# Decays of a gated DeltaNet kept head by head in DRAM and broadcast into the decay tiles themselves

## The chip, the cores and the metric

The kernel runs on one core of one Trainium2 chip. The metric is the device time of one execution in microseconds (us), the median of several runs. The core has a matrix engine (TensorE, PE in the rows), a vector engine (VectorE, DVE), a scalar engine (ScalarE, ACT), GpSimd (POOL) and SyncE (SP), which here only issues transfers; ACT issues some too (ACTq). Each engine works through its own list of instructions in a fixed order, and an instruction that waits holds up everything behind it in that list.

## The reference, cut to what matters

One encoder layer: a SwiGLU feed-forward block, a mixer, a second feed-forward block. The change lies in the mixer's branch B, a gated DeltaNet with 8 heads, run in both directions. Per head and direction the decays `g` are summed up inside each chunk, and the chunk matrices are weighted with the exponential of differences of these sums:

```python
g = jnp.cumsum(g, axis=-1)
decay = jnp.exp(jnp.where(incl, g[..., :, None] - g[..., None, :], -jnp.inf))
a_mat = jnp.where(strict, jnp.einsum('bhnid,bhnjd->bhnij', k_beta, k) * decay, 0.0)
attn = jnp.einsum('bhnid,bhnjd->bhnij', q, k) * decay
```

So each head needs, for 2 directions and 4 chunks of 128 positions, the sums once as a column (one per partition) and once as a row that all 128 partitions hold.

## The kernel before, in words

The sequence has T = 512 positions, the width is 1024. Every product is split into three matrix passes of 128x512 (lines 186, 187, 188: `hi` times `uh`, `lo` times `uh`, `hi` times `ul`), so that a weight tile `raw` comes by a transfer (line 169), is rounded to `hi` by ACT (line 174) and its rest `lo` made by DVE (line 176). Three `raw` tiles and three pairs `hi`, `lo` are in rotation.

In the mixer, the eight heads are built by the generator `build`, which `EMIT`, a table of steps, interleaves with the other generators (scan, place, gates); heads are counted below by the order of their decay transfers. The tile framework then orders the instructions by priority, so that each engine's list is fixed when the program is built. `build(hd)` goes through these steps:

- three projections with short convolution (line 444 on DVE): `cq`, `ck`, `cv`;
- SiLU to `qT`, `kT`, `vT` (ACT), and the transfer of the decay rows: `Gb`, 128 x 8 x 128, one buffer (lines 468, 469);
- `tok`: transposes on PE into the bank `tp` (line 479), of which there is one; ACT empties it (lines 481, 484);
- `st`, small columns: lines 514 and 516 on DVE read the last element of each row of `Gb`, and line 517 (ACT) takes the exponential;
- `ef` and `eb`, the decay matrices of the two directions: line 528 on DVE subtracts the column from `Gb` (eight instructions of 128x128), then ACT (lines 531 to 533) and, for `eb`, POOL (line 534);
- PE makes `k k^T` and `k q^T` in the bank `o`, again one, two chunks at a time (lines 547, 548); DVE multiplies with the decay matrices into `nl` (line 552) and `at` (line 556). The second two chunks on PE must wait until `at` has read the first two out of `o`.

The row form of the decays comes from `grow` in DRAM: G is transposed on PE to `gt`, 64 rows of 128 (direction, chunk, head), and stored by one transfer (line 424) in the middle of the mixer's start. `Gb` of a head reads eight pieces of 512 bytes out of it for every partition. SP's list holds the weights, `Gb`, and the transfers of the triangular inverse (`dl`, `A`, `da`, `t`).

Of the kernel before, what the change touches and what calls it, by code (L numbers as in the profile page):

```python
# [7 lines left out]
F32 = mybir.dt.float32  # L8
# [8 lines left out]
P = 128  # L17
# [5 lines left out]
NC = T // P  # L23
H = 8
# [29 lines left out]
def tile_layer(  # L54
# [23 lines left out]
    nc = tc.nc  # L78
    pe, act, dve, pool = nc.tensor, nc.scalar, nc.vector, nc.gpsimd

    def open_pool(stack, name, bufs=1, **kw):
        if "space" not in kw:
            kw["reuse_waits"] = "tile"
        return stack.enter_context(tc.tile_pool(name=name, bufs=bufs, **kw))
# [27 lines left out]
    h = open_pool(first, "big", side="right").tile([P, KT, T], F32, tag="big", name="h")  # L112
# [206 lines left out]
    def mixer(st, u, h, post):  # L319
# [3 lines left out]
        scr = open_pool(st, "scr", bufs=2, space=DRAM)  # L323
# [10 lines left out]
        def project(i):  # L334
            made.add(i)
            if i in early:
                return early[i]
            ps = bank()
            product(ps, weight(w_in[i], KT), u, 0, KT, True, True)
            return ps  # L340
# [3 lines left out]
        wk = open_pool(dn, "wk", bufs=2)  # L344
        one = open_pool(dn, "one", bufs=1)
        with ExitStack() as dd:
            beta = dnc.tile([P, NC, 16], F32, name="beta")
            G = dnc.tile([P, 2, NC, H], F32, name="G")
# [17 lines left out]
            def early_half(t0, t1):  # L366
                for i, w in ew.items():
                    if t0 == 0:
                        early[i] = bank()
                    product(early[i], w, u, 0, KT, True, True, t0, t1)  # L370
# [15 lines left out]
            x = dt.tile([P, NC, 16], F32, tag="spx", name="spx")  # L386
# [21 lines left out]
            for d in range(2):  # L408
                dve.scalar_tensor_tensor(
                    out=g[:, d], in0=x[:, :, d * H : d * H + H], scalar=-1.0,  # L410
# [9 lines left out]
            pe.transpose(ps[0:64, 0:P], G[:].rearrange("p d c h -> p (d c h)"), ident[:])  # L420
            gt = dt.tile([64, P], F32, tag="gt", name="gt")
            act.copy(gt[:], ps[0:64, 0:P])
            grow = scr.tile([2 * NC, H, P], F32, tag="grow", name="grow")
            nc.sync.dma_start(grow[:].rearrange("a h p -> (a h) p"), gt[:])
            early_half(T // 2, T)

        with dn:
# [8 lines left out]
            def taps(acc, src, w, n):  # L436

                mid = n // 2
                act.activation(out=acc[:], in_=src[:], func=ACT.Copy, scale=w[:, mid : mid + 1])  # L439
                for i in range(n):  # L440
                    o = i - mid
                    lo, hi = max(0, -o), T - max(0, o)
                    if o:
                        dve.scalar_tensor_tensor(out=acc[:, lo:hi], in0=src[:, lo + o : hi + o],  # L444
                                                 scalar=w[:, i : i + 1], in1=acc[:, lo:hi], op0=ALU.mult,
                                                 op1=ALU.add)

            def short_conv(i):

                ps = project(12 + i)  # L450
                acc = cp.tile([P, T], F32, tag="cacc", name="cacc")
                taps(acc, ps, cvd_sb[:, i], 5)
                return acc

            def build(hd, s):
                cq = short_conv(hd)
                yield
                ck = short_conv(8 + hd)
                yield
                cv = short_conv(16 + hd)  # L460
                yield
# [3 lines left out]
                act.activation(out=kT[:], in_=ck[:], func=ACT.Silu)  # L465
                vT = cv
                act.activation(out=vT[:], in_=cv[:], func=ACT.Silu)
                Gb = wk.tile([P, 8, P], F32, tag="Gb", bufs=1, name="Gb")
                nc.sync.dma_start(Gb[:], grow[:, hd, :].unsqueeze(0).to_broadcast([P, 8, P]))

                yield

                ss = slot.tile([P, 2, NC], F32, tag="ss", name="ss")
# [28 lines left out]
                ns, sb, nr, wj, el = (st_[:, 2], st_[:, 3, 0:NC], st_[:, 4], st_[:, 5], st_[:, 6])  # L502
# [8 lines left out]
                dve.tensor_mul(brk, beta[:, :, hd], rk)  # L511
                for d in range(2):
                    last = (P - 1, 0)[d]
                    dve.tensor_sub(wj[:, d * NC : d * NC + NC], Gb[:, d * NC : d * NC + NC, last],
                                   G[:, d, :, hd])
                    dve.tensor_copy(el[:, d * NC : d * NC + NC], Gb[:, d * NC : d * NC + NC, last])
                act.activation(out=wj, in_=wj, func=ACT.Exp)
                act.activation(out=el, in_=el, func=ACT.Exp)

# [1 line left out]

                yield

                ef = wk.tile([P, NC, P], F32, tag="E", bufs=2, name="ef")
                eb = wk.tile([P, NC, P], F32, tag="E", bufs=2, name="eb")
                for d, m, op in ((0, ef, ALU.add), (1, eb, ALU.min)):
                    for c in range(NC):
                        dve.tensor_scalar(out=m[:, c, :], in0=Gb[:, d * NC + c, :],
                                          scalar1=G[:, d, c, hd : hd + 1], scalar2=0.0, op0=ALU.subtract,
                                          op1=op)  # L530
                act.activation(out=ef[:], in_=ef[:], func=ACT.Abs)
# [9 lines left out]
                for c2 in range(2):  # L541
                    ps = bank("o", psx)
                    pk = ps[:].rearrange("p (c z x) -> p c z x", c=2, z=2)
                    for i in range(2):
                        c = 2 * c2 + i
# [3 lines left out]
                    for i in range(2):  # L549
                        c = 2 * c2 + i  # L550
# [265 lines left out]
            def advance(t):  # L816


                kind, i = t[0], int(t[1:] or 0)
                if kind == "y" and (len(made) < 60 or not away):  # L820
                    return
                if kind in fill:
                    if kind == "m":
                        for x in fill["a"]:
                            pass
                        for x in ("s3", "s4"):
                            while not done(x):
                                advance(x)
                    next(fill[kind], None)
                    return  # L830
                if t not in live:
                    g = i if kind == "i" else [i in x for x in GROUPS].index(True)
                    before = {"b": [], "i": [f"b{x}" for x in GROUPS[g]], "p": [f"p{i - 2}"] * (i > 1) + [f"i{g}"],
                              "s": [f"s{i - 2}"] * (i > 1) + [f"p{i}"]}[kind]
                    for x in before:
                        while not done(x):
                            advance(x)
                    if kind == "i":
                        inverses[i] = invert([S[x] for x in GROUPS[i]])
                        live[t] = None  # L840
                        return
                    live[t] = {"b": lambda: build(i, S[i]), "s": lambda: scan(i, S[i]),
                               "p": lambda: place(i % 2, S[i], inverses[g], GROUPS[g].index(i))}[kind]()
                if live[t] is not None and next(live[t], fill) is fill:
                    live[t] = None
# [114 lines left out]
    with ExitStack() as st:  # L960
        u, h, ssum = mixer(st, u2, h, ctx)
# [81 lines left out]
```

## Time and profile before

| | |
|---|---|
| median of 3 runs | 1385.83 us (1382.4 to 1386.79) |
| the profiled execution: its own time | 1384.16 us |
| its span, first to last instruction | 1382.1 us |
| mean granted TensorE clock | 0.992 of full speed |
| PE busy | 97% of the span |
| DVE, ACT, POOL busy | 58%, 41%, 5% |
| DMA moved | 193.46 MB, mean 140 GB/s |

The span is what the trace shows; around it lie 2.1 us of the execution's own time. An engine that is busy 97% sets the time wherever its idle time and its slow stretches do not. The rows further down give for each stretch how long an engine was busy, what it waited for, and at which share of full speed the chip let the matrix engine run (granted clock: 1.00 is 2.4 GHz, 0.50 is 1.2 GHz).

### The profile page before, as it was taken

To read this page: it belongs to the slowest core of one execution; us is meant where nothing else is said; L and a number is where in the kernel's file an instruction comes from. 1 tells how busy PE (TensorE), PEld (TensorE's weight loads), DVE (VectorE), ACT (ScalarE), POOL (GpSimd) and SP (SyncE) were. 2 spreads that over 40 slices of the span, in tenths; PEclk is the share of its full clock that TensorE was granted. 3 is DMA by queue.
4 is the path that set the end of the run, shared out by engine and by line. 5 is a ranking of instruction groups with operands and counts; after the bars stand their busy time and mean duration, and the time that the engine had idled before them with its cause. 6 is when DMAs were issued, how large, how long until landed. Compare 5 with 4: busy or idle time off the path is not lost.

```text
span 1382.1 us, 19594 instructions
## 1 busy us (share of the span) xinstructions
PE 1339.7 (97%) x7417; PEld 1112.8 (81%) x7417; DVE 804.8 (58%) x1745; ACT 566.4 (41%) x1150; POOL 64.1 (5%) x103
## 2 busy tenths in 40 slices
PE   6999999999998899999999999999999999999997
PEld 4888888888887778778777787888798888888886
DVE  6865555555375778786864785647553444443333
ACT  3333333322256664467555334545433333332330
POOL 0000000000000100021112001000000000000000
PEclk9999999999999999999999999999999999999999
DMA  8656566555434443333541433557503334333332
GB/s 319 218 159 191 181 193 191 171 172 182 130 126 94 124 130 127 121 116 107 130 139 60 124 113 95 168 197 245 176 31 104 125 109 134 124 108 95 100 100 71
DMA packets 86591, 193.46 MB, mean 140 GB/s; under 512 B 24737, under 2 KB 35169, under 8 KB 86370
## 3 DMA queue, kind: packets, MB, share of 16 engines
q1 hardware_dynamic: 71008, 164.29, 38.6%
q10 hardware_dynamic: 15490, 27.94, 5.9%
q8 instruction: 58, 0.95, 0.3%
q14 instruction: 35, 0.29, 0.1%
HBM read 171.19 MB, written 21.00 MB: 139 GB/s over the span
## 4 chain that ended last, share of the span: by engine, by line
PE 80%; DMA 8%; DVE 5%; issue 3%; ACT 3%; POOL 1%; ACTq 0%; POOLq 0%; SPq 0%; DVEq 0%
PE acc L188 22%; PE acc L186 22%; PE acc L187 22%; DMA msb<-gtd 2%; DMA Gb<-grow 2%; PE acc L918 1%; DVE lo L176 1%; PE ch L674 1%; PE ch L918 1%; PE o L697 1%; PE ch L685 1%; DMA raw<-w_in 1%; DVE cacc L444 1%; PE tp L610 1%; ACT hi L174 1%
## 5 line engine op out<-in xcount | busy, mean ns | idle before, releaser
L186 PE MATMUL acc<-uh,hi 128*128 128x512 f32 (+1 forms) x1224 | 473.3, 387 | 2.0 <-DVE sps L397 0.9
L187 PE MATMUL acc<-uh,lo 128*128 128x512 f32 (+1 forms) x1224 | 473.8, 387 | 0.7 <-DVE lo L176 0.7
L188 PE MATMUL acc<-ul,hi 128*128 128x512 f32 (+1 forms) x1224 | 472.3, 387 | 0.0
L174 ACT CAST hi<-raw 128x512 fp32r<-128x512 f32 (+1 forms) x416 | 252.2, 612 | 535.1 <-PE acc L188 479.0
L176 DVE TENSOR_TENSOR lo<-raw,hi 128x512 fp32r<-128x512 f32 (+1 forms) x416 | 280.4, 681 | 293.1 <-ACT hi L174 291.7
L186 PEld LDWEIGHTS acc<-uh,hi 128*128 128x128 f32 x1224 | 231.2, 189 | 44.4 <-ACT cacc L439 1.1
L187 PEld LDWEIGHTS acc<-uh,lo 128*128 128x128 f32 x1224 | 231.2, 189 | 42.3 <-DVE lo L176 1.3
L188 PEld LDWEIGHTS acc<-ul,hi 128*128 128x128 f32 x1224 | 230.8, 189 | 41.2
L186 PE MATMUL acc<-gh,hi 128*128 128x512 f32 (+1 forms) x396 | 144.9, 366 | 0.0
L187 PE MATMUL acc<-gh,lo 128*128 128x512 f32 (+1 forms) x396 | 144.6, 365 | 0.0
L188 PE MATMUL acc<-gl,hi 128*128 128x512 f32 (+1 forms) x396 | 144.4, 365 | 0.0
L150 DVE SCALAR_TENSOR_TENSOR raw<-raw,cs 128x1024 f32<-128x1024 f32 x72 | 87.9, 1223 | 59.8 <-DMA raw<-w_ada 59.7
L187 PEld LDWEIGHTS acc<-gh,lo 128*128 128x128 f32 x396 | 74.4, 188 | 12.1
L186 PEld LDWEIGHTS acc<-gh,hi 128*128 128x128 f32 x396 | 74.4, 188 | 12.1
L188 PEld LDWEIGHTS acc<-gl,hi 128*128 128x128 f32 x396 | 74.4, 188 | 12.1
L444 DVE SCALAR_TENSOR_TENSOR cacc<-acc,cvd_sb,cacc 128x510 f32<-128x510 f32 (+1 forms) x96 | 71.1, 742 | 4.3 <-ACT cacc L439 3.8
L313 DVE TENSOR_TENSOR sa<-sa,acc 128x512 f32<-128x512 f32 x40 | 27.4, 685 | 34.9 <-PE acc L188 33.2
L228 POOL TENSOR_TENSOR rs<-ms,mhalf 128x2 f32<-128x2 f32 (+1 forms) x7 | 6.2, 887 | 840.1 <-DVE ms L225 840.1
L196 ACT CAST gh<-sa 128x512 fp32r<-128x512 f32 x44 | 27.4, 622 | 18.4 <-DVE sa L313 13.7
L197 DVE TENSOR_TENSOR gl<-sa,gh 128x512 fp32r<-128x512 f32 x44 | 30.3, 692 | 5.5 <-PE tp L918 2.1
L206 ACT ACTIVATE sq<-h 128x512 f32<-128x512 f32 (+1 forms) x25 | 14.1, 563 | 47.3 <-DVE h L255 46.9
L584 DVE TENSOR_TENSOR A<-A,tmp 96x30 f32<-96x30 f32 (+29 forms) x90 | 29.0, 322 | 1.5
(270 smaller groups left out, 1454.4 us busy)
## 6 DMA issues: line engine op xcount, KB each, us to landing
raw<-w_ada SPq DMA_DIRECT2D x72, 512.0 KB
raw<-w_in SPq DMA_DIRECT2D x60, 512.0 KB
raw<-w2u SPq DMA_DIRECT2D x44, 512.0 KB
raw<-w1u SPq DMA_DIRECT2D x36, 512.0 KB
raw<-w1d SPq DMA_DIRECT2D x16, 512.0 KB
raw<-w2d SPq DMA_DIRECT2D x16, 512.0 KB
wf<-w1f SPq DMA_DIRECT2D x8, 512.0 KB
Gb<-grow SPq DMA_DIRECT2D x8, 512.0 KB
```

The source lines that it names most:

```text
L150: dve.scalar_tensor_tensor(out=raw[:], in0=raw[:], scalar=1.0, in1=cs[:], op0=ALU.mult, op1=ALU.mult, accum_out=part[:, n : n + 1])
L174: act.copy(hi[:], raw[:, k : k + n, :])
L176: dve.tensor_sub(lo[:], raw[:, k : k + n, :], hi[:].bitcast(F32))
L186: pe.matmul(ps[:, t0:t1], wh, rh[:, k0 + k, t0:t1], start=a, stop=False)
L187: pe.matmul(ps[:, t0:t1], wl, rh[:, k0 + k, t0:t1], start=False, stop=False)
L188: pe.matmul(ps[:, t0:t1], wh, rl[:, k0 + k, t0:t1], start=False, stop=b)
L196: act.copy(hi, src)
L197: dve.tensor_sub(lo, src, hi.bitcast(F32))
L313: dve.tensor_mul(sa[:], sa[:], ps[1][:])
L444: dve.scalar_tensor_tensor(out=acc[:, lo:hi], in0=src[:, lo + o : hi + o], scalar=w[:, i : i + 1], in1=acc[:, lo:hi], op0=ALU.mult, op1=AL ...
L584: dve.tensor_tensor(out=A[:, j + 1 : 32, 0:j], in0=A[:, j + 1 : 32, 0:j], in1=tv, op=ALU.add)
L918: pe.matmul(early[m][:], terms[i][0][:, m, :], terms[i][1], start=k == 0 and i == 0, stop=k == KT - 1 and i == 2)
```

## The change

`grow` is laid out head first: `[8 heads, 2 directions, 512 positions]` instead of `[8 direction-chunks, 8 heads, 128]`. A head's row of one direction is then one piece of 2 KB. `build` no longer has `Gb`. It allocates the two decay tiles `ef` and `eb` itself, now four buffers (two heads) instead of two, right after `ck`, two steps earlier than `Gb` was loaded, and loads each by one transfer that broadcasts the 2 KB to all partitions. Line 528 then subtracts in place. The buffer space is the same: four tiles of 2 KB per partition against `Gb` of 4 KB and two of 2 KB.

```diff
-            grow = scr.tile([2 * NC, H, P], F32, tag="grow", name="grow")
-            nc.sync.dma_start(grow[:].rearrange("a h p -> (a h) p"), gt[:])
+            grow = scr.tile([H, 2, NC * P], F32, tag="grow", name="grow")
+            nc.sync.dma_start(grow[:].rearrange("h d (c p) -> (d c) h p", p=P), gt[:])
...
                 ck = short_conv(8 + hd)
+
+                E = [wk.tile([P, NC, P], F32, tag="E", bufs=4, name=x) for x in ("ef", "eb")]
+                for d in range(2):
+                    nc.sync.dma_start(E[d][:].rearrange("p a b -> p (a b)"),
+                                      grow[hd, d : d + 1, :].to_broadcast([P, NC * P]))
                 yield
...
-                Gb = wk.tile([P, 8, P], F32, tag="Gb", bufs=1, name="Gb")
-                nc.sync.dma_start(Gb[:], grow[:, hd, :].unsqueeze(0).to_broadcast([P, 8, P]))
...
-                    dve.tensor_sub(wj[:, d * NC : d * NC + NC], Gb[:, d * NC : d * NC + NC, last],
-                                   G[:, d, :, hd])
-                    dve.tensor_copy(el[:, d * NC : d * NC + NC], Gb[:, d * NC : d * NC + NC, last])
+                    dve.tensor_sub(wj[:, d * NC : d * NC + NC], E[d][:, :, last], G[:, d, :, hd])
+                    dve.tensor_copy(el[:, d * NC : d * NC + NC], E[d][:, :, last])
...
-                ef = wk.tile([P, NC, P], F32, tag="E", bufs=2, name="ef")
-                eb = wk.tile([P, NC, P], F32, tag="E", bufs=2, name="eb")
+                ef, eb = E
                 for d, m, op in ((0, ef, ALU.add), (1, eb, ALU.min)):
                     for c in range(NC):
-                        dve.tensor_scalar(out=m[:, c, :], in0=Gb[:, d * NC + c, :],
+                        dve.tensor_scalar(out=m[:, c, :], in0=m[:, c, :],
                                           scalar1=G[:, d, c, hd : hd + 1], scalar2=0.0, op0=ALU.subtract,
                                           op1=op)
```

SP's list where the first three heads' decays are loaded, before (a tile's number tells its copies apart; behind a row stands what it waits for, DMAHW being the earlier transfers):

```order
L424 DMA grow_3256<-gt_3254 64x128 [waits Activation_49]
L469 DMA Gb_3366<-grow_3256 128x8x128 [waits DMAHW4_49]
L169 DMA raw_3767<-w_in 128x1024 [waits DMAHW6_49,DMAHW0_49,DVE_49]
L469 DMA Gb_3662<-grow_3256 128x8x128 [waits DMAHW5_49,DVE_49]
L169 DMA raw_3808<-w_in 128x1024 [waits DMAHW1_49,DVE_49]
L169 DMA raw_3872<-w_in 128x1024 [waits DMAHW3_49,DVE_49]
L169 DMA raw_3949<-w_in 128x1024 [waits DMAHW6_49,DMAHW2_49,DVE_49]
L568 DMA dl_4088<-nl_3429 128x1024 [waits DVE_49]
L574 DMA A_4092<-dl_4088 8x32x32 [waits DMAHW3_49]
L169 DMA raw_3990<-w_in 128x1024 [waits DMAHW0_49,DVE_49]
L469 DMA Gb_3917<-grow_3256 128x8x128 [waits DMAHW7_49,DVE_49]
```

The same place now:

```order
L424 DMA grow_3256<-gt_3254 8x8x128 [waits Activation_49]
L462 DMA ef_3355<-grow_3256 128x512 [waits DMAHW4_49]
L462 DMA eb_3356<-grow_3256 128x512 [waits DMAHW6_49]
L169 DMA raw_3771<-w_in 128x1024 [waits DMAHW0_49,DVE_49]
L462 DMA ef_3575<-grow_3256 128x512
L462 DMA eb_3576<-grow_3256 128x512 [waits DMAHW1_49]
L169 DMA raw_3812<-w_in 128x1024 [waits DMAHW2_49,DVE_49]
L169 DMA raw_3876<-w_in 128x1024 [waits DMAHW3_49,DVE_49]
L169 DMA raw_3951<-w_in 128x1024 [waits DMAHW7_49,DVE_49]
L568 DMA dl_4092<-nl_3429 128x1024 [waits DMAHW5_49,DVE_49]
L462 DMA ef_3766<-grow_3256 128x512 [waits DMAHW6_49,DVE_49]
L462 DMA eb_3767<-grow_3256 128x512 [waits DVE_49,Pool_49]
```

The second head's pair no longer waits for DVE, and the third head's pair, whose buffers are the first head's, now stands right behind the store `dl` of the first head's `nl`, ahead of a weight, instead of behind it.

DVE's list at the first head's decays, before:

```order
L176 TENSOR_TENSOR lo_3621<-raw_3617,hi_3619 128x512 [waits DMAHW1_49,Activation_49]
L514 TENSOR_TENSOR st_3397<-Gb_3366,G_3041 128x4 [waits DMAHW5_49]
L516 COPY st_3397<-Gb_3366 128x4
L514 TENSOR_TENSOR st_3397<-Gb_3366,G_3041 128x4
L516 COPY st_3397<-Gb_3366 128x4
L528 TENSOR_SCALAR ef_3415<-Gb_3366,G_3041 128x128 x4
L528 TENSOR_SCALAR eb_3416<-Gb_3366,G_3041 128x128 x4
```

and now (the numbers of `raw`, `hi`, `lo` have moved by 4; lines 514, 516 are now 516, 517):

```order
L516 TENSOR_TENSOR st_3399<-ef_3355,G_3041 128x4 [waits DMAHW5_49]
L517 COPY st_3399<-ef_3355 128x4
L528 TENSOR_SCALAR ef_3355<-ef_3355,G_3041 128x128 [waits DVE_49]
L528 TENSOR_SCALAR ef_3355<-ef_3355,G_3041 128x128
L176 TENSOR_TENSOR lo_3625<-raw_3621,hi_3623 128x512 [waits DMAHW1_49,Activation_49]
L516 TENSOR_TENSOR st_3399<-eb_3356,G_3041 128x4 [waits DMAHW6_49]
L517 COPY st_3399<-eb_3356 128x4
L528 TENSOR_SCALAR ef_3355<-ef_3355,G_3041 128x128 x2
L528 TENSOR_SCALAR eb_3356<-eb_3356,G_3041 128x128 [waits DVE_49]
L528 TENSOR_SCALAR eb_3356<-eb_3356,G_3041 128x128 x3
```

The wait for `ef` now stands ahead of a weight's `lo`, the one for `eb` behind it.

PE's list at the third head's second two chunks, before (they are the rows of `o_4076`; 27 product passes lie between them and the first two chunks):

```order
L188 MATMUL acc_4227<-ul_522,hi_4234 128x512
L186 MATMUL acc_4359<-uh_521,hi_4362 128x512 [waits DVE_49,Activation_49]
L187 MATMUL acc_4359<-uh_521,lo_4364 128x512 [waits DVE_49]
L188 MATMUL acc_4359<-ul_522,hi_4362 128x512
L547 MATMUL o_4076<-kT_3914 128x128 [waits DVE_49,PE_49]
L548 MATMUL o_4076<-qT_3912,kT_3914 128x128
L547 MATMUL o_4076<-kT_3914 128x128
```

and now (rows of `o_4080`):

```order
L188 MATMUL acc_4231<-ul_522,hi_4238 128x512
L186 MATMUL acc_4231<-uh_521,hi_4238 128x512
L187 MATMUL acc_4231<-uh_521,lo_4240 128x512
L547 MATMUL o_4080<-kT_3918 128x128 [waits DVE_49,PE_49]
L548 MATMUL o_4080<-qT_3916,kT_3918 128x128
L547 MATMUL o_4080<-kT_3918 128x128
L548 MATMUL o_4080<-qT_3916,kT_3918 128x128
```

They have moved 10 product passes forward; 17 are left ahead of them. The order differs in other places too, above all after the inverse of the first three heads.

## Rows read from the trace of the kernel before

**Rows 1.** The page: busy time, share of the span and instructions

```profile
PE 1339.7 (97%) x7417; PEld 1112.8 (81%) x7417; DVE 804.8 (58%) x1745; ACT 566.4 (41%) x1150; POOL 64.1 (5%) x103
```

**Rows 2.** The chain that ended last, shares by line

```profile
PE acc L188 22%; PE acc L186 22%; PE acc L187 22%; DMA msb<-gtd 2%; DMA Gb<-grow 2%; PE acc L918 1%; DVE lo L176 1%; PE ch L674 1%; PE ch L918 1%; PE o L697 1%; PE ch L685 1%; DMA raw<-w_in 1%; DVE cacc L444 1%; PE tp L610 1%; ACT hi L174 1%
```

**Rows 3.** Waits in 425 to 515 us: total, times, longest

```profile
PE o L547 <- DVE at L556: 6.4, 2, 3.4
PE tp L479 <- ACT junk L484: 4.2, 1, 4.2
...
DVE st L514 <- DMA Gb<-grow: 13.2, 3, 5.7
```

**Rows 4.** Timeline of PE: start, us, instruction [idle before <-releaser]

```profile
437.24 0.39 PE L186 MATMUL acc<-uh,hi 128*128 128x512 f32 x1
441.78 1.12 PE L479 MATMUL tp<-ident,cacc 128*128 128x128 f32 x4 [4.15 <-ACT junk L484]
...
478.36 0.77 PE L547 MATMUL o<-kT 128*128 128x128 f32 x2 [3.43 <-DVE at L556]
...
506.07 0.76 PE L547 MATMUL o<-kT 128*128 128x128 f32 x2 [2.96 <-DVE at L556]
```

**Rows 5.** Windows: stretch, us, busy by engine, granted clock, DMA share, GB/s

```profile
441.78:447.39 5.61, 5.61 (x16) 4.55 (x16) 4.57 (x6) 4.47 (x7) 0.64 (x1) 0.50 0.38 81
...
478.36:481.49 3.13, 3.13 (x12) 2.84 (x12) 1.12 (x4) 0.67 (x3) 0.06 (x1) 0.50 0.28 84
...
506.07:509.06 2.99, 2.99 (x11) 2.76 (x12) 1.60 (x5) 1.87 (x4) 0.06 (x1) 0.53 0.64 192
```

**Rows 6.** Timeline of DVE

```profile
429.88 0.74 DVE L444 SCALAR_TENSOR_TENSOR cacc<-acc,cvd_sb,cacc 128x510 f32<-128x510 f32 x1
...
438.34 0.17 DVE L514 TENSOR_TENSOR st<-Gb,G 128x4 f32<-128x4 f32 x1 [5.66 <-DMA Gb<-grow]
...
458.19 0.41 DVE L556 TENSOR_TENSOR at<-o,eb 128x256 f32<-128x256 f32 x1
...
474.29 0.17 DVE L514 TENSOR_TENSOR st<-Gb,G 128x4 f32<-128x4 f32 x1 [3.91 <-DMA Gb<-grow]
...
498.10 0.17 DVE L514 TENSOR_TENSOR st<-Gb,G 128x4 f32<-128x4 f32 x1 [3.62 <-DMA Gb<-grow]
```

**Rows 7.** Timeline of ACT

```profile
433.30 1.28 ACT L517 ACT_TABLE_LOAD   x1
438.69 0.21 ACT L517 ACTIVATE st<-st 128x8 f32<-128x8 f32 x1 [4.10 <-DVE st L514]
```

**Rows 8.** The chain in order of time, its transfers: start, us from issue to landing

```profile
426.44 1.83 DMA grow<-gt
428.29 10.03 DMA Gb<-grow
...
489.27 8.80 DMA Gb<-grow
...
827.52 3.45 DMA t<-da
...
946.25 2.94 DMA msb<-gtd
```

**Rows 9.** Windows, columns as in rows 5

```profile
434.00:436.00 2.00, 2.00 (x10) 1.63 (x10) 0.00 (x0) 0.59 (x1) 0.00 (x0) 1.00 1.03 77
...
470.00:472.00 2.00, 2.00 (x14) 1.82 (x13) 0.38 (x1) 1.51 (x3) 0.00 (x0) 1.00 0.33 73
```

**Rows 10.** Windows of the mixer, columns as in rows 5

```profile
425.00:515.00 90.00, 78.91 (x360) 64.41 (x359) 61.95 (x172) 55.59 (x128) 7.89 (x12) 0.92 0.45 120
515.00:580.00 65.00, 65.00 (x319) 53.59 (x318) 52.42 (x122) 26.89 (x44) 2.30 (x2) 1.00 0.42 130
580.00:720.00 140.00, 138.33 (x1127) 112.21 (x1125) 105.46 (x340) 90.81 (x232) 23.83 (x39) 1.00 0.43 121
720.00:910.00 190.00, 186.72 (x1430) 151.32 (x1429) 120.25 (x325) 83.87 (x225) 20.67 (x31) 1.00 0.38 115
```

## The prediction

> **What bounds the kernel now.** I read the page first: PE is busy 97% of the span [rows 1], so the time is PE's work plus what PE idles plus what it loses at the lower clock, and a change that takes no work from PE can gain only in the latter two. The chain that ended last, by line, is next: beside the matrix passes the largest entries are two transfers at 2% each, and one of them is `Gb<-grow` [rows 2]. So the buffer that goes is on the path, and I looked for the place. The windows of the mixer say where: between 425 and 515 us PE is busy 78.9 of 90 us at a mean granted clock of 0.92; in 515 to 580 it does not idle at all, in 580 to 720 it idles 1.7 of 140 us, in 720 to 910 3.3 of 190 [rows 10]. Only the first of these stretches has something to give.
>
> The waits of that stretch name three links [rows 3]. DVE waits three times for `Gb`, 13.2 us in all. PE waits twice for DVE's `at` (6.4 us) and once for ACT's `junk` (4.2 us). The timelines join them. DVE's three waits end at 438.34, 474.29 and 498.10 [rows 6]; PE's three end 3.4 to 8 us after these, at 441.78 (4.15 us idle), 478.36 (3.43) and 506.07 (2.96) [rows 4]. In the first case ACT stands between: its table load is done at 433.30 + 1.28 = 434.58, then it waits 4.10 us for the small columns that DVE makes from `Gb` [rows 7], and the squares that free PE's bank `tp` stand behind that wait. In the other two cases DVE's late `at` holds the bank `o`. After each of these waits PE runs at about half clock: 5.61 us at 0.50, 3.13 at 0.50, 2.99 at 0.53 [rows 5], so a `Gb` wait is paid twice.
>
> **The change part by part.** *What can be won.* Idle time: 4.15 + 3.43 + 2.96 = 10.5 us. Clock: a stretch of L us at share c would take L x c at full clock, so 5.61 x 0.50 + 3.13 x 0.50 + 2.99 x 0.47 = 2.8 + 1.6 + 1.4 = 5.8 us. Together 16.3 us. All of it hangs on `Gb`; PE's own work is unchanged.
>
> *How long the new transfers take.* None of their form is in the trace of before, so I bound them. `Gb` takes 10.03 us for the first head and 8.80 for the fourth [rows 8]. It is 512 KB in 1024 pieces of 512 bytes. Two transfers of the same 32 KB differ by their pieces alone: `grow<-gt`, 64 pieces, lands in 1.83 us, `t<-da`, 256 pieces of 128 bytes, in 3.45 [rows 8]. That is 8 ns for a piece more, and 1024 pieces at that price make about 8 us more than 64 do: just `Gb`. So the count of pieces, not the bytes, seems to set it. `ef` and `eb` have 128 pieces each, of 2 KB; the nearest row is `msb<-gtd`, also 128 pieces of 2 KB, 2.94 us at its quickest [rows 8]. The bounds for the pair are thus 2.9 and 10.0 us; I take 4.5, near the row of the same form, since two go out one after the other.
>
> The Trainium skill (DMA: Bandwidth & Descriptors, Specifications) speaks against this step: it puts the smallest transfer at line rate at 512 bytes, and by that the pieces of `Gb` were large enough already, and longer ones land no sooner. With the pair at 10.0 us the sum would be 8.2 us instead of 14.8, the second rival below. The trace does not agree: in 434 to 436 us, where hardly anything but `Gb` moves, the DMA engines are taken up fully (1.03) for 77 GB/s [rows 9].
>
> *First head.* `grow` lands at 428.3 as before, so nothing moves ahead of that. The pair is issued then and is there by 432.8 instead of 438.3. DVE is free of its line 444 at about 430.6 [rows 6] and now waits for `ef` ahead of a weight's `lo`, some 1 us instead of 5.66. ACT needs the columns at 434.58, when its table is loaded; DVE has them a few tenths after `eb`. So the pair may take up to 5.9 us before anything is late. From its exponential to PE's start ACT has 441.78 - 438.69 = 3.09 us of work; 434.58 + 3.09 = 437.67, and PE's last pass began at 437.24 and takes 0.39 [rows 4]. The gap closes to 0.04 us. I leave 0.3.
>
> *Second head.* Its pair no longer waits for buffers of the first and goes out right behind it. It caused no wait of its own before and causes none now.
>
> *Third and fourth head.* The four buffers let these pairs go out when `at` of the head two before is done, at 458.19 + 0.41 = 458.6 for the third [rows 6], on the clock of before, and the third head's `Gb` landed at 474.3. With 4.5 us it lands at 463.1, with 10.0 at 468.6, both long before DVE asks (474.29 - 3.91 = 470.4; one part of the new list asks some 5 us sooner, still behind 463.1). Both later waits of DVE go, whichever bound holds. What replaces them: four to five subtractions of line 528 stand before the third head's `at` now; 0.2 us for that. PE's second `o` of the third head stands 10 passes further ahead, so DVE has 17 passes' time instead of 27; at 10 passes in 2 us [rows 9] that is 3.4 us for one set of `nl`, two `at`, a `lo` and a line 444. It fits, barely; I leave 1.0 us.
>
> *The rest.* Line 528 in place is the same eight instructions of the same shape per head, on DVE, in time that is hidden under PE; if that cover went, it would be nothing more either. SP issues eight transfers more, all hidden: SP mostly waits for weight buffers. `E` wait for `at` stands ahead of a weight on SP (the `dl`, `ef`, `eb`, `A`, weight order), but `at` is right behind `nl`, which `dl` waits for anyway, so the weight loses under 1 us against three buffers of lead. `grow` is stored in the same 64 pieces.
>
> Left over: 0.3 + 0.2 + 1.0 = 1.5 us. Sum: 16.3 - 1.5 = 14.8 us. The profiled execution took 1384.16 us, so 1369.4; its time lies 1.67 us under the median shown, and on the median's scale that is 1385.83 - 14.8 = **1371.0 us**.
>
> **The rivals.** A change under 0.3% (4.2 us) can hardly be told from none in this kernel.
>
> *The broadcast is bound by bytes or by its one source.* `Gb` moves 73 GB/s in 470 to 472 us too, at a third of the engines' share [rows 9], so something other than the engines may set its pace: 128 partitions read the same few KB, and the new pair does that too. Then `eb` lands at 438.3 again, the first wait stays whole (4.15 + 2.81 us), the other two go by the earlier issue. Gain 16.3 - 7.0 - 1.2 = 8.2 us, time 1377.6. For it: the equal rates; against it: 64 and 256 pieces of the same bytes.
>
> *The time is given back in the same stretch.* With 15 us less, DVE's 62.0 us and ACT's 55.6 [rows 10] fill 82% and 74% of it, both with an order that waits. In 515 to 580 DVE fills 81% and PE does not idle, but ACT only 41%; in 580 to 720 it is 75% and 65% for 1.7 us idle. If ACT or DVE trails, short waits come back, each with its half clock. Two waits of the size of today's (some 12 us with clock) leave about 3: time 1383.
>
> *The decay tiles hold up the weights (slower).* From the third head on, SP stops at `ef` until `at` of the head two before is done, with weights behind it. If `at` comes later than PE needs that weight, PE stands, 4.4 to 7 us each time with its clock, as in rows 4 and 5. Six heads could do it; it takes three to use up the gain and four to be slower by over 0.3%: about 1391. Against it: `at` follows `nl` directly in the code, and `dl` in front waits for `nl` already.
>
> **How the numbers follow.** The forecast 0.60, the broadcast bound by its source 0.15, given back 0.14, weights held up 0.11. The first two are faster by over 0.3%: 0.75; the third is the same: 0.14; the fourth slower: 0.11. Range 1366 to 1384: below, all 16.3 us (1369.5) and the 3.3 us that PE idles in 720 to 910, where the order changes as well; above, it takes in the second rival at 1377.6 and the third at 1383, and leaves out the fourth. The forecast's own range is 1368 to 1375.
>
> **What would show it.** Right: no wait of DVE for `ef` or `eb` over 1.5 us; `ef` landing 3 to 4 us after issue; PE busy over 97% between 425 us and the point that was 515, the granted clock near 1.00 there, and the stretch 14 to 16 us shorter; from there to the end the same lengths within 2 us. Wrong step by step: a first wait of 4 us at the squares (the transfer's length), PE waiting for `at` at the third head (the order), short waits of PE on `hi` or `lo` (given back), SP's waits at `ef` with weights late behind (buffers). The prediction is wrong as a whole if the three waits go and the mixer after 515 us grows by as much.

## The result and the profile after

The changed kernel takes 1375.07 us in the median of five executions (1368.65 to 1377.27), the kernel before 1385.37: a ratio of 0.993, 95% interval 0.9905 to 0.9955. In another set of runs (run e4 below) it was 1372.28 against 1385.75, 0.9908 (0.9887 to 0.993). So it is faster, by 10.3 and 13.5 us between the medians. The profiled execution of after took 1377.27 us, with a span of 1375.3; that is 6.8 us under the span of before.

The page of the changed kernel: busy time by engine, and the chain that ended last, by line. PE's work is that of [rows 1], and `Gb`, 2% in [rows 2], is gone from the chain; no row of `ef` or `eb` takes its place.

```profile
PE 1340.2 (97%) x7417; PEld 1114.0 (81%) x7417; DVE 804.2 (58%) x1745; ACT 566.7 (41%) x1150; POOL 64.9 (5%) x103
...
PE acc L188 21%; PE acc L186 21%; PE acc L187 21%; DMA msb<-gtd 1%; PE acc L918 1%; DMA raw<-w_in 1%; DMA raw<-w2u 1%; PE ch L674 1%; DVE lo L176 1%; PE ch L685 1%; PE ch L918 1%; PE o L697 1%; PE tp L610 1%; PE tp L481 1%; PE ch L668 1%
```

Its waits in 425 to 515 us, against [rows 3]: DVE's 13.2 us for `Gb` have become 1.5 us for `ef`, and PE's three waits (twice for `at`, 6.4 us together, once for `junk`, 4.2 us) no longer show.

```profile
DVE st L516 <- DMA ef<-grow: 1.5, 1, 1.5
```

Its windows, columns as in [rows 10] (stretch, us, busy PE, PEld, DVE, ACT, POOL, granted clock, DMA share, GB/s). In the first stretch PE is busy 89.84 us instead of 78.91, and the clock is 1.00 instead of 0.92. The second and third stretches went the other way: PE idles 1.5 + 3.8 us where it idled 0 + 1.7, and the clock in 580 to 720 us is 0.96.

```profile
425.00:515.00 90.00, 89.84 (x441) 74.62 (x440) 73.47 (x199) 69.44 (x147) 10.09 (x14) 1.00 0.47 146
515.00:580.00 65.00, 63.48 (x402) 51.39 (x401) 53.47 (x140) 28.57 (x66) 4.46 (x8) 1.00 0.37 114
580.00:720.00 140.00, 136.25 (x1043) 110.13 (x1041) 96.66 (x306) 78.92 (x201) 20.70 (x31) 0.96 0.39 116
720.00:910.00 190.00, 186.87 (x1394) 152.01 (x1391) 119.89 (x324) 83.80 (x222) 20.29 (x30) 1.00 0.39 120
```

PE's timeline names the places (start, us, instruction [idle before <- releaser]), and short windows the clock around the last two:

```profile
577.19 0.46 PE L674 MATMUL ch<-vt,nl 128*128 128x128 f32 x2 [1.13 <-DVE nl L650]
...
620.52 0.50 PE L187 MATMUL acc<-uh,lo 128*128 128x512 f32 x1 [1.43 <-DVE lo L176]
...
653.76 0.33 PE L724 MATMUL tp<-ident,on 128*128 128x128 f32 x1 [1.12 <-DVE on L719]
...
654.98 0.33 PE L724 MATMUL tp<-ident,on 128*128 128x128 f32 x1 [0.89 <-DVE on L719]
```

```profile
620.00:625.00 5.00, 4.48 (x19) 3.90 (x20) 4.03 (x9) 2.04 (x4) 0.00 (x0) 0.67 0.51 145
...
655.00:660.00 5.00, 5.00 (x28) 3.73 (x29) 2.99 (x11) 0.02 (x1) 0.00 (x0) 0.58 0.51 153
660.00:665.00 5.00, 5.00 (x23) 4.21 (x23) 3.62 (x13) 3.06 (x10) 0.00 (x0) 0.74 0.18 65
```

That is the ledger of this execution. Won in 425 to 515 us: 10.9 us of idle time and the 5.8 us of clock that the prediction worked out. Given back: 3.6 us of idle time, and in the three windows above 5 x (0.33 + 0.42 + 0.26) = 5.0 us of clock. That leaves 8.1 us; the spans differ by 6.8. Most of the rest lies further on: behind a wait that both kernels have, the clock fell once more, which cost 5 x 0.34 = 1.7 us in before (first row) and 5 x (0.47 + 0.21) = 3.4 us in after (the other two).

```profile
1000.00:1005.00 5.00, 4.79 (x29) 4.49 (x28) 2.03 (x6) 0.91 (x2) 0.69 (x1) 0.66 0.00 0
```

```profile
990.00:995.00 5.00, 4.99 (x23) 4.74 (x24) 0.42 (x2) 0.42 (x1) 0.70 (x1) 0.53 0.00 0
995.00:1000.00 5.00, 5.00 (x36) 5.00 (x36) 3.59 (x9) 2.24 (x5) 0.00 (x0) 0.79 0.00 0
```

The chain in order of time says what stood ahead of the wait at 620 us. The two exponentials of the small columns (lines 518, 519) are parted by a SiLU (line 468); the three rows of 1.28 us are table loads. The squares of the scan (line 713) come among them, and behind these the power on POOL, the scaling `on`, and the weight's `lo` that PE waits for.

```profile
609.11 1.28 ACT L518
...
611.11 1.28 ACT L468
...
613.83 1.28 ACT L519
...
616.96 0.30 ACT junk L713 x2
...
617.59 1.02 POOL rr L717
...
619.20 0.67 DVE on L719 x3
619.87 0.61 DVE lo L176
```

### The profile page after: what moved, and what is told of

Its sections match the earlier page's. It is cut to its first block, busy times and chain, and to the rows that moved or that the text cites. A ratio compares the mean times of both kernels' runs of the same rounds, so it can differ in the third digit from the quotient of the medians.

```text
span 1375.3 us, 19612 instructions
## 1 busy us (share of the span) xinstructions
PE 1340.2 (97%) x7417; PEld 1114.0 (81%) x7417; DVE 804.2 (58%) x1745; ACT 566.7 (41%) x1150; POOL 64.9 (5%) x103
## 4 chain that ended last, share of the span: by engine, by line
PE 79%; issue 8%; DMA 5%; DVE 4%; ACT 3%; POOL 1%; ACTq 0%; POOLq 0%; DVEq 0%; SPq 0%
PE acc L188 21%; PE acc L186 21%; PE acc L187 21%; DMA msb<-gtd 1%; PE acc L918 1%; DMA raw<-w_in 1%; DMA raw<-w2u 1%; PE ch L674 1%; DVE lo L176 1%; PE ch L685 1%; PE ch L918 1%; PE o L697 1%; PE tp L610 1%; PE tp L481 1%; PE ch L668 1%
## 5 line engine op out<-in xcount | busy, mean ns | idle before, releaser
L196 ACT CAST gh<-sa 128x512 fp32r<-128x512 f32 x44 | 27.4, 622 | 18.6 <-DVE sa L313 13.9
```

Source lines behind the costliest of these rows:

```text
L196: act.copy(hi, src)
```

## The experiments

The first theory (A) had two parts: the pieces' count made `Gb` late, and the new order gave time back. The rivals: bytes or the one source set the transfer's length; a mixer without these waits loses the time in any order. Runs e1, e2 and e4, with the kernel before beside them on the same chip, cross the two kinds of transfer with the two orders.

**e1: the old order with long pieces.** In the kernel before, only:

```diff
-            grow = scr.tile([2 * NC, H, P], F32, tag="grow", name="grow")
-            nc.sync.dma_start(grow[:].rearrange("a h p -> (a h) p"), gt[:])
+            grow = scr.tile([1, H, 8 * P], F32, tag="grow", name="grow")
+            nc.sync.dma_start(grow[:].rearrange("a h (r p) -> (a r) h p", p=P), gt[:])
...
-                nc.sync.dma_start(Gb[:], grow[:, hd, :].unsqueeze(0).to_broadcast([P, 8, P]))
+                nc.sync.dma_start(Gb[:].rearrange("p (a r) x -> p a (r x)", r=8),
+                                  grow[:, hd, :].unsqueeze(0).to_broadcast([P, 1, 8 * P]))
```

> The kernel before with one thing changed: grow lies head first, so that Gb (one buffer, loaded at its old place, by one transfer) is read in 128 pieces of 4 KB instead of 1024 of 512 bytes. Every engine's list has the same order as before, row by row. Theory A (the count of pieces sets the length of the transfer, and the new order gave time back later): Gb lands 3 to 4 us after issue, the three waits of DVE for Gb shrink below 1 us each even with one buffer (they were 3.6 to 5.7 us, and the transfer gets some 5.5 us shorter), and since the order after 515 us is that of before, nothing is given back: 14 to 16 us faster, 1369 to 1372, ahead of the changed kernel. Rival B (what was given back is not the order's: a mixer without these waits runs into ACT and DVE anyhow): the three waits go, but 5 to 9 us come back between 560 and 670 us here too: about 1375, like the changed kernel. Rival C (bytes or the one source set the length): Gb still takes 8 to 10 us and the time is that of before, within 3 us.

Measured: 1367.12 us, ratio 0.9872 (0.9849 to 0.9894): 18.6 us faster than before. One buffer, loaded at its old place, is enough to end all three waits, and the time after 515 us is kept:

```profile
425.00:515.00 90.00, 89.66 (x438) 74.22 (x437) 72.24 (x195) 66.42 (x145) 10.19 (x14) 1.00 0.45 141
515.00:580.00 65.00, 64.58 (x403) 51.98 (x402) 53.60 (x138) 27.55 (x62) 4.46 (x8) 1.00 0.41 130
580.00:720.00 140.00, 138.59 (x1171) 113.12 (x1170) 100.47 (x322) 89.76 (x225) 21.07 (x33) 1.00 0.39 118
```

**e2: the new order with the old layout.** In the changed kernel, `grow` as before:

```diff
-                    nc.sync.dma_start(E[d][:].rearrange("p a b -> p (a b)"),
-                                      grow[hd, d : d + 1, :].to_broadcast([P, NC * P]))
+                    nc.sync.dma_start(E[d][:],
+                                      grow[d * NC : d * NC + NC, hd, :].unsqueeze(0).to_broadcast([P, NC, P]))
```

> The changed kernel with the old layout of grow: four decay tiles and the early issue stay, but each of the two transfers of a head reads 512 pieces of 512 bytes. Every engine's list has the same order as in the changed kernel. Theory A: by 8 ns for a piece each transfer takes 5 to 6 us alone and the pair 9 to 10, so DVE waits some 5 us for eb of the first head and PE loses the first stall with its clock (7 us) as before, while the waits of the third and fourth head are gone (9.3 us); from this goes what the changed kernel gives back between 560 and 670 us (5 to 9 us): within 4 us of the kernel before, 1380 to 1385. Rival C (the length is set by bytes or source): the same time as the changed kernel, within 2 us. A third case (buffering alone did it): no wait at the first head either, and the time of the changed kernel.

Measured: 1381.41 us, 0.9963 (0.995 to 0.9977). The first head waits as before, the later heads do not (DVE in 425 to 515 us; the second `ef` wait is 0.4 us), and what is given back after 515 us stays: PE idles 5.3 us in 515 to 720 us. The first row is from the chain: `eb` takes 9.29 us for half of `Gb`'s bytes, behind `ef`.

```profile
429.12 9.29 DMA eb<-grow
```

```profile
DVE st L516 <- DMA ef<-grow: 4.1, 2, 3.7
PE tp L481 <- ACT junk L486: 3.3, 1, 3.3
DVE st L516 <- DMA eb<-grow: 2.4, 1, 2.4
```

**e4: the changed kernel again**, unedited, on the same chip.

> The changed kernel once more, on the same chip as the other three, so that all four corners (pieces of 512 bytes or longer, old or new order) are compared on one chip. All theories: 1373 to 1377, 8 to 12 us faster than before. What it also tells is whether the short waits of PE near 570, 620 and 655 us belong to the order, and so stand at the same instructions again, or change from one execution to the next.

Measured: 1372.28 us, 0.9908 (0.9887 to 0.993). PE's waits stand at the same instructions with the same lengths, but the clock behind them does not fall; the same windows as above:

```profile
577.29 0.46 PE L674 MATMUL ch<-vt,nl 128*128 128x128 f32 x2 [1.13 <-DVE nl L650]
...
620.59 0.50 PE L187 MATMUL acc<-uh,lo 128*128 128x512 f32 x1 [1.44 <-DVE lo L176]
...
652.23 0.33 PE L724 MATMUL tp<-ident,on 128*128 128x128 f32 x1 [1.13 <-DVE on L719]
```

```profile
655.00:660.00 5.00, 5.00 (x40) 3.81 (x39) 4.01 (x17) 2.87 (x10) 0.00 (x0) 1.00 0.73 211
660.00:665.00 5.00, 5.00 (x32) 3.94 (x31) 4.71 (x16) 2.43 (x10) 0.00 (x0) 1.00 0.38 100
```

So the 3.6 us of idle time belong to the order, and the 5 us of clock come or not by the execution. Between e1 and e4 the order differs, with the buffers and the early load that belong to it; the transfers are quick in both: 5.2 us between the medians.

**e3: one exponential.** In the changed kernel, lines 518 and 519 as one:

```diff
-                act.activation(out=wj, in_=wj, func=ACT.Exp)
-                act.activation(out=el, in_=el, func=ACT.Exp)
+                act.activation(out=st_[:, 5:7], in_=st_[:, 5:7], func=ACT.Exp)
```

> The changed kernel with the two exponentials of the small columns (lines 518 and 519, 128x8 each) made as one of 128x16. Elsewhere the order moves a little with it. Theory A, in its narrow form (the time given back near 610 and 645 us comes from two table loads that a SiLU between these two exponentials costs, 2 x 1.28 us at each of the two places, ahead of the squares that PE's next work hangs on): PE's idle time near 620 and 655 us goes, with the half clock after it: 4 to 6 us faster than the changed kernel, 1369 to 1371. Rival B (any order of this mixer has such places): other short waits of PE with half clock turn up between 560 and 720 us, and the time is that of the changed kernel within 2 us.

Measured: 1373.53 us, 0.991 (0.989 to 0.9929): that of e4. The repair did not work, and so does not decide: a table load for line 532 (at 615.08 us) now falls among the squares, so that three loads stand ahead of their end as before.

**e7 and e8: without the SiLU in between**, in the changed kernel and in that of e1:

```diff
-                act.activation(out=qT[:], in_=cq[:], func=ACT.Silu)
+                act.activation(out=qT[:], in_=cq[:], func=ACT.Copy)
```

> The changed kernel with the SiLU of qT (line 468) replaced by a copy of the same shape, which needs no table of its own: qT is then the convolution without its activation. This takes away the table loads that come between the two exponentials (24 loads in ACT's list instead of 33), at the price of some movement in the order. Theory A, narrow form (the extra table loads ahead of the squares are what makes PE wait near 620 and 653 us in the new order): those two waits go with the half clock after them, and the time comes within 2 us of the kernel with long pieces and the old order that has the same replacement; 4 to 6 us gained on the changed kernel. Rival B (the waits come from the order of the other engines): the waits stay, gain under 2 us.

> Control to the run before: the kernel with long pieces, Gb and the old order, with the SiLU of qT replaced by a copy as well (26 loads instead of 33). Theory A, narrow form: in the old order the loads cost PE next to nothing (one wait of 1 us at 650), so this gains under 2 us on the kernel with long pieces, 1365 to 1367. Rival (fewer table loads help any order alike): 4 us or more gained here too.

Measured: 1370.44 us, 0.9906 (0.9882 to 0.9931), and 1369.97 us, 0.9903 (0.9877 to 0.9929). The two meet, as theory A had it, but not where it had it: the changed kernel gains nothing that can be told, and e8 is no faster than e1 by its median. Whether it is slower is not shown: the ratios are 0.9903 and 0.9872, from two sets of runs, with intervals that overlap, and e8's profiled execution has the shorter span (1364.6 against 1366.5 us). Both orders move with the edit. In e7's trace one table load is left ahead of the squares at 610 us, and PE's wait for `lo` there is gone, but 1.19 us at `tp` remain near 650, and others come up; from 515 to 720 us PE idles 4.0 us, against 5.3 in the changed kernel, 1.8 in e1 and 2.7 in e8. The loads explain at most a part.

**e6: the early load undone.** In the changed kernel, the two tiles are allocated and loaded behind the SiLUs again:

```diff
                 ck = short_conv(8 + hd)
-
-                E = [wk.tile([P, NC, P], F32, tag="E", bufs=4, name=x) for x in ("ef", "eb")]
...
                 act.activation(out=vT[:], in_=cv[:], func=ACT.Silu)
+                E = [wk.tile([P, NC, P], F32, tag="E", bufs=4, name=x) for x in ("ef", "eb")]
...
```

> The changed kernel with the early issue undone: the two tiles are allocated and loaded where Gb was, behind the three SiLUs; four buffers, 2 KB pieces and the subtraction in place stay. On ACT's list the exponentials of the small columns are split by a SiLU at the same two places as in the changed kernel. Theory A (with long pieces the transfer is short enough at either place, and what is given back hangs on the order of the in-place form, not on the load's place): the time of the changed kernel within 2 us, and the same short waits of PE near 577, 620 and 653 us. Rival (the early issue is worth something by itself): waits of DVE for ef or eb between 465 and 500 us come back, 3 us or more slower than the changed kernel.

Measured: 1372.56 us, 0.9914 (0.9889 to 0.9939): the changed kernel's time, with its waits (1.14 us at 576.53, 1.43 at 619.84, 1.13 and 0.89 at 651 to 653). The early issue is worth nothing that can be told once the transfer is quick.

**e5: short pieces near one another.** The last open point was the cause of the quick transfer. The kernel before, `grow` head first, a gap of 64 bytes behind every 512:

```diff
-            grow = scr.tile([2 * NC, H, P], F32, tag="grow", name="grow")
+            grow = scr.tile([H, 2 * NC, P + 16], F32, tag="grow", name="grow")
...
-                nc.sync.dma_start(Gb[:], grow[:, hd, :].unsqueeze(0).to_broadcast([P, 8, P]))
+                nc.sync.dma_start(Gb[:], grow[hd, :, 0:P].unsqueeze(0).to_broadcast([P, 8, P]))
```

> The kernel before with grow laid out head first, as in the run with long pieces, but with a gap of 64 bytes behind every 512, so that Gb is still read in 1024 pieces of 512 bytes, now out of 4.6 KB instead of 29 KB. Every engine's list is that of before. Theory A (the count of pieces sets the length): Gb lands 9 to 10 us after issue as before, all three waits of DVE stay, and the time is that of before within 3 us. Rival (what made the long pieces quick is that a head's rows lie together in DRAM): Gb lands in 4 to 5 us and the time is that of the run with long pieces, 14 to 18 us faster.

Measured: 1365.82 us, 0.9866 (0.9837 to 0.9895). Theory A falls in its first part. The page of e5 (first row) has 86583 packets, 35161 of them under 2 KB, as good as before (86591 and 35169), where the long pieces of e1 make 79415; and DVE has its columns at 433.16 us, 4.8 us after the issue at 428.41:

```profile
DMA packets 86583, 193.46 MB, mean 142 GB/s; under 512 B 24729, under 2 KB 35161, under 8 KB 86362
```

```profile
433.16 0.17 DVE L514 TENSOR_TENSOR st<-Gb,G 128x4 f32<-128x4 f32 x1 [0.54 <-DMA Gb<-grow]
```

**e9 to e12: the distance of the pieces.** In the kernel before a head's eight pieces lie 8 heads x 512 = 4096 bytes apart. e9 keeps the old layout with a gap of 64 bytes (4608 apart); e10, e11, e12 are e5 with wider gaps (4096, 2048, 1024). Each reads 1024 pieces of 512 bytes a head, in the order of before.

The edit of e9 to the kernel before, and that of e10 to e5 (512 and 256 in place of 1024 in e11 and e12):

```diff
-            grow = scr.tile([2 * NC, H, P], F32, tag="grow", name="grow")
+            grow = scr.tile([2 * NC, H, P + 16], F32, tag="grow", name="grow")
...
-                nc.sync.dma_start(Gb[:], grow[:, hd, :].unsqueeze(0).to_broadcast([P, 8, P]))
+                nc.sync.dma_start(Gb[:], grow[:, hd, 0:P].unsqueeze(0).to_broadcast([P, 8, P]))
```

```diff
-            grow = scr.tile([H, 2 * NC, P + 16], F32, tag="grow", name="grow")
+            grow = scr.tile([H, 2 * NC, 1024], F32, tag="grow", name="grow")
```

> The kernel before, grow in its old order (direction and chunk first, head second), but with a gap of 64 bytes behind every 512, so that the eight pieces of a head lie 4608 bytes apart instead of 4096. 1024 pieces of 512 bytes, out of 32 KB, every engine's list as before. The count of pieces is out as a cause by now. Theory P (the distance of exactly 4096 bytes between the eight pieces, which all partitions read, makes the transfer slow): Gb lands in 4 to 6 us, the three waits go and the time is that of the long pieces, 14 to 18 us faster than before. Rival L (a head's rows have to lie near one another): Gb takes 9 to 10 us as before, and the time is that of before within 3 us.

> The kernel before with grow head first, as in the run with near pieces, but each 512 bytes followed by a gap of 3584, so that a head's eight pieces lie 4096 bytes apart again. Theory P: Gb takes 9 to 10 us as before, the three waits of DVE are back, and the time is that of before within 3 us. Rival L (nearness): the same, since 29 KB are spanned; but together with the run at 4608 it tells the two apart. A third case (what counts is that the head's rows are not among those of other heads): quick, 14 to 18 us faster.

> The same with a distance of 2048 bytes between the eight pieces of a head (15 KB spanned). Theory P, if only the distance of 4096 does it: 4 to 6 us for Gb, no waits. If distances of a power of two grow worse step by step: 6 to 8 us, the first wait shrinks to 1 to 3 us and the later two go, 8 to 14 us faster than before. Rival L (nearness): between the runs at 576 and at 4096 too, 6 to 8 us.

> The same with a distance of 1024 bytes between the eight pieces of a head (7.5 KB spanned). Both theories: close to the run with near pieces (576 bytes apart), Gb in 4 to 6 us, 14 to 18 us faster than before. What it tells beside the others is whether the length falls in steps from 4096 over 2048 to 1024, or at once.

| bytes between pieces | run | first `Gb`, us | time, us | ratio to before |
|---|---|---|---|---|
| 576 | e5 | 4.8 | 1365.82 | 0.9866 (0.9837 to 0.9895) |
| 1024 | e12 | 4.4 | 1367.39 | 0.9865 (0.9835 to 0.9895) |
| 2048 | e11 | 6.34 | 1372.08 | 0.99 (0.9865 to 0.9935) |
| 4096 | e10 | 9.63 | 1386.19 | 1.0007 (0.9989 to 1.0024) |
| 4096 | before | 10.03 | see above | 1 |
| 4608 | e9 | 4.3 or less | 1368.17 | 0.9878 (0.984 to 0.9916) |
| none (4 KB pieces) | e1 | 4.1 or less | 1367.12 | 0.9872 (0.9849 to 0.9894) |

Each ratio is to the kernel before in the same set of runs. The lengths run from SP's issue to the landing in the chain or, where the chain lacks it, to DVE's first read (at 432.96 us in e12, 433.54 in e9, 433.32 in e1, the last two without a wait). The chain's rows of e10, and then of e11:

```profile
428.65 9.63 DMA Gb<-grow
464.78 9.81 DMA Gb<-grow
489.62 9.30 DMA Gb<-grow
```

```profile
429.15 6.34 DMA Gb<-grow
459.22 7.10 DMA Gb<-grow
479.85 5.61 DMA Gb<-grow
```

The fourth head's landing stands in the chain of nearly every run, that of e1 and e9 too (rows in this order): 5.33 us in 128 long pieces, 5.38 in 1024 pieces 4608 bytes apart. It is 5.82 us in e5, 5.61 in e11, 9.30 in e10 and 8.80 in before.

```profile
477.84 5.33 DMA Gb<-grow
```

```profile
478.06 5.38 DMA Gb<-grow
```

The window 430 to 432 us, where SP has issued the first `Gb` (at 428.6 to 429.2) and one weight (at 430.1 to 430.9), in e10, e11, e12 and e9 in this order: the last column climbs from 88 to 135, 234 and 251 GB/s. Before has 71 there, e5 175, with its weight issued at 429.9; so the column sets 4096 and 2048 bytes apart from the others, and does not rank those.

```profile
430.00:432.00 2.00, 1.99 (x11) 1.38 (x10) 0.79 (x2) 1.99 (x4) 0.00 (x0) 1.00 0.37 88
```

```profile
430.00:432.00 2.00, 2.00 (x10) 1.47 (x8) 1.29 (x3) 1.99 (x3) 0.00 (x0) 1.00 0.48 135
```

```profile
430.00:432.00 2.00, 1.99 (x11) 1.38 (x10) 0.75 (x2) 1.99 (x5) 0.00 (x0) 1.00 0.88 234
```

```profile
430.00:432.00 2.00, 2.00 (x10) 1.68 (x9) 1.56 (x3) 1.99 (x3) 0.00 (x0) 1.00 0.92 251
```

e9 decides against nearness: its pieces span more than those of before and are quick. e10 decides against the head-first layout as such: it is as slow as before. What makes the broadcast slow is the distance of 4096 bytes; 2048 does it in part, 6.34 and 7.10 us for the first and third head, but at the fourth, with 5.61, no more than the others. The Trainium skill (DMA: Bandwidth & Descriptors, Latency and other measured facts) reports the like for row pitches of 2 MiB and more, with a pad of 4 KiB as the cure and one of 192 bytes as none; it calls the cause, several streams that meet in one memory channel, an inference. Its pitch lies between the rows of different partitions; here all partitions read the same eight pieces. Here the pitch is a five-hundredth of that, and 512 bytes more cure it (64 behind each of the eight rows of a group). The cause inside the memory is not shown here either.

## Why the prediction was right, and where its reasons were wrong

Predicted were 1371.0 us and a gain of 14.8; measured are 1375.07 and 10.3, in the second set 13.5.

**Where the time is lost: right.** Three waits of DVE, three of PE with their lower clock, 16.3 us in 425 to 515 us. e1 leaves every list as it was and makes only the transfer quick: its span is 1382.1 - 1366.5 = 15.6 us shorter.

**The length of the new transfers: right in size, wrong in reason.** `ef` was there 3.6 us after its issue (432.20 - 428.60), `eb` at the latest at 433.48 instead of the 432.8 that was worked out. But "the count of pieces, not the bytes, seems to set it" fell: 1024 pieces take 9.6 to 10.0 us or 4.3 to 4.8 by their distance alone. Piece count is worth next to nothing: 5.33 us in 128 pieces, 5.38 in 1024, at the fourth head (e1, e9). The step went wrong where two transfers of 32 KB [rows 8] were read as a price per piece and stretched to 1024 pieces; that the sum came out at just `Gb` looked like a proof. The rule of the Trainium skill (DMA: Bandwidth & Descriptors, Specifications) that 512 bytes are enough, which the prediction weighed and set aside, agrees with e1 and e9. The rival built on it failed all the same, since the new layout took away the distance along with the short pieces; no step of the prediction looked at the distance, so that was luck. The sign by which the rule was set aside, DMA engines taken up fully (1.03 in [rows 9]), does not go with the slow broadcast: in e10, where `Gb` is as slow, they are busy 0.21 in the same window.

```profile
434.00:436.00 2.00, 2.00 (x10) 1.68 (x9) 0.00 (x0) 0.76 (x1) 0.00 (x0) 1.00 0.21 54
```

**Third and fourth head: right, twice over.** Four buffers and the early issue end their waits but for 0.4 us with slow transfers (e2), and quick transfers alone end them but for 0.2 us with one buffer at the old place (e1). No run has the four buffers alone. The 1.5 us set down as left over were too many: PE idles 0.16 us in that stretch. The 17 passes ahead of the third head's second `o` last 4.1 us there, not the 3.4 that the prediction read, and that is enough.

**The rest, put at nothing: the term that was mis-sized.** The order after 515 us was taken to cost 0 to 2 us. It costs 3.6 us of idle time in both profiled executions of the changed kernel (PE idles 5.3 us in 515 to 720 in the first, 5.2 in e4, against 1.7 in before, 1.8 in e1), and 5.0 us of clock in the first, none in e4. The rival "given back" had the right kind of loss, short waits with a lower clock, but put it into 425 to 515 us, where there was none. Shown is that the idle time goes with the order: PE's 7417 matmuls stand in one order in before, e1, e5 and e9 to e12, and in another in the changed kernel, e2, e4 and e6. These last have the loss, e1 does not; it hangs neither on the layout (e1, e2) nor on the load's place (e6). Which rows of that order cause it stays open: the table loads are the nearest cause in the chain, yet taking them away brought PE's idle time down by only a third of the difference and the time by nothing that can be told.

**Weights held up: not seen.** No step of the chain after 515 us is a transfer of `ef` or `eb`, and none of PE's waits of that stretch that are shown above ends on a transfer.

The best version is the smallest edit: the kernel before with 64 bytes of gap in `grow` (e5, e9) or with `grow` head first (e1). These take 1365.8 to 1368.2 us, 1.2 to 1.3% less than the kernel before; the buffer need not go. Beside the changed kernel, on one chip, only e1 was run, 5.2 us ahead of it (e4).

## What to carry to other kernels

Where a transfer of small rows runs at a fraction of its neighbours' rate, look at the distance of its rows in DRAM before counting its pieces, and pad one row to see. When an edit changes a layout and the order at once, undo each alone: here the first was worth more than the whole. A price for an operation read from two rows should not be stretched to four times their range without a third.

## What was not expected of the hardware

The distance of the pieces: 4608 bytes give 4.3 us or less for the first head, 4096 give 9.6 to 10.0, 2048 give 6.3, for the same 512 KB in the same 1024 pieces. And the granted clock: behind the same waits of PE, 1.12 and 0.89 us, it fell to 0.58 and 0.74 in one execution of the changed kernel (655 to 665 us) and stayed at 1.00 in another, which is most of the 5.9 us between their spans (1375.3 and 1369.4).
